# A hybrid decoder layer: the row statistics of the first norm from a second reading of x, another order for the first tile, and three biases on ScalarE

## The chip, the cores and the metric

The kernel runs on one core of one Trainium2 chip. The core has five engines with a queue each, and every engine works through its queue in order: PE (TensorE, matrix products), DVE (VectorE), ACT (ScalarE), POOL (GpSimd) and SP (SyncE, which here only issues transfers). PEld is PE's loading of the stationary operand, which overlaps its products. The metric is the time of one execution on the device, in microseconds (us). Lines such as L1411 are lines of the kernel before.

## The reference

One layer of a causal decoder trunk, sequence 1024, model width 1024, float32. Only the first part matters here:

```python
mod = silu(c) @ W_ada + b_ada            # shift, scale, gate for each of two sub-layers
y = x * rsqrt(mean(x * x, axis=-1) + EPS) * g_mix
u = y * (1 + scale1) + shift1
proj = u @ w_in                          # q, k, v, u_ssm, two gates
```

Behind it follow dilated window attention over eight heads, a state space branch, gates, an output projection, a second modulated norm, a convolutional gated MLP and a final norm.

## The kernel before

Everything is kept transposed: channels on the 128 partitions, tokens along the row. `xs[k]` (k = 0 to 7) is tile k of x, 128 channels by 1024 tokens, and `halves` are its two halves of 512 tokens. Precision comes from splitting each operand into a high and a low part (`xg[k][:, 0]` and `xg[k][:, 1]`, the same for weights): `mm3` (L186 to L188) is three products, high by high, high by low, low by high.

The first stage does not wait for the norm's root. A tile of x needs only its gain `gs1`, which a dot of a row block of `w_ada` with silu(c) gives (`row_dot`, `ada_dot`, DVE, L1427). So loop `k` (L395) multiplies the unnormed, scaled tile by the columns of four weight tiles (first q, first k, two of the state space input) into seven PSUM banks `b0`: seven `mm3` per k, 21 products. `prep_a(k)` makes the gain and ACT's high part (L323), `prep_b(k)` DVE's low part (L376); both run one and two tiles ahead. The root comes in later, when `scale_r` multiplies the banks by `rr` (L432), the reciprocal root of the mean square, held on all partitions.

That root is built here from `square(k)` (ACT, L350), summed over the tiles by DVE (L352), and from `stats(h2)` (L381): a product with a matrix of -1 sums over the partitions and spreads the sum to all of them, and `rsqrt_of` takes the root on ACT with one Newton step on DVE (L1395 to L1400), for 512 tokens at a time. The first half is done inside tile 7, the second in the V stage.

The shift needs eight more dots (row blocks 0 to 7, loaded late, L402), then `shl` (L448 to L450), and PE's products for a bias row (L458, L459). The bias is added to the scaled banks by POOL (`add_bias0`, L483). The V stage (L537 to L576) then makes `u` per tile and half: `mod_a` is DVE then ACT (L1405, L1406), `mod_b` DVE (L1411). Its first half covers tokens 0 to 511 for all eight k, its second half the rest, and between the products of the second half the first q and k parts are split (`put_q`, `put_k`), V is stored (`put_v`), and the next weights are split (`Weights`, ACT L122 and POOL L123).

The order is written out by hand: the program order of each engine is the order of the calls below, and waits are put in where data or a buffer is needed. `late` says before which (tile, bank) of the loop a step is called. All loads go through SP's queue, in the order of the calls; a load waits for its buffer, and everything behind it waits as well. Pages of 8 KB per partition (`b.A`, 17 of them) hold rows of `w_ada`, `xg`, `u` and more. Before the loop PE runs `WARM` dummy products (L281).

Of the kernel before, what the change touches and what calls it, by code (L numbers as in the profile page):

```python
# [10 lines left out]
F32 = mybir.dt.float32  # L11
# [37 lines left out]
QHI = ((-5, -3, 0, 2, 3, 5, 6), (-7, -5, -2, 0, 12, 2, 17))  # L49
EPS = 1e-6  # L50
BIG = 1e30
WARM = 26
DOTS = ((5, 3), (5, 6), (6, 1), (6, 3), (7, 2), (7, 2), (7, 3), (7, 5))
STATS = ((7, 0),)
NEWTON = ((7, 2),)
A2PACE, A2AHEAD, A2DELAY = 8.0, 2, 0.0
LEAD, FILL_PACE, SCORE_PACE = 9, 1.55, 1.2
SLOW_PACE, LAST_PACE, SLOW_END = 1.52, 0.5, 60
# [152 lines left out]
def body(tc, I, O, dbg=None):  # L211
    b = Builder(tc, I, O)
    nc = tc.nc
    with ExitStack() as ctx:
# [87 lines left out]

        def split_w(i):
            raw = raws.pop(i)
            w = b.whl.tile([P, 2, 1024], R32, name="whl", tag="whl") if i in (0, 1, 5) else b.A([P, 2, 1024], R32, "whA")
            for cs in halves if i == 0 else [slice(0, 1024)]:
                nc.scalar.activation(w[:, 0, cs], raw[:, cs], AF.Copy)
                nc.vector.tensor_sub(w[:, 1, cs], raw[:, cs], w[:, 0, cs].bitcast(F32))
                if i == 0:
                    xg_hi(0, [halves[1]] if cs.start == 0 else [])  # L310
            return w

        def split_hi(i):
# [21 lines left out]
        for k in range(3):  # L335
            load_x(k)
        nc.sync.dma_start(spar, I["spar"])
        sqp = b.A([P, 2, S], F32, "sq")
        b0 = {k: b.ps(tag) for k, tag in zip(((1, 0), (2, 0), (0, 0), (3, 0), (1, 1), (2, 1), (0, 1)),
                                             ("s", "s", "t", "t", "mm", "mm", "o"))}  # L340
        w0, xg = [], {}

        base = pg1.tile([P, KT], F32, name="base")
        nc.vector.tensor_scalar(base, cols[:, KT:2 * KT], 1.0, None, op0=OP.add)
        lag1 = []

        def square(k):

            sq = sqp[:, 1 if k else 0]
            nc.scalar.activation(sq, xs[k], AF.Square)  # L350
            if k:
                lag1.append(lambda: nc.vector.tensor_add(sqp[:, 0], sqp[:, 0], sq))  # L352

        def prep_a(k):
            low = None
            if k and k % 2 == 0:
                w, low = split_hi(k // 2)
                w0.append(w)
            row_dot(KT + k)
            nc.vector.tensor_scalar(gs1[:, k:k + 1], mod[:, KT + k:KT + k + 1], base[:, k:k + 1],  # L360
                                    cols[:, C_GMIX + k:C_GMIX + k + 1], op0=OP.add, op1=OP.mult)
            if k == 0:
                xg_hi(0, halves[:1])
                w0.append(split_w(0))
            else:
                xg_hi(k, [slice(0, S)])
            if low:
                low()
            for fn in lag1:
                fn()  # L370
            lag1.clear()
            square(k)

        def prep_b(k):
            for hs in halves if k == 0 else [slice(0, S)]:
                nc.vector.scalar_tensor_tensor(xg[k][:, 1, hs], xs[k][:, hs], gs1[:, k:k + 1],  # L376
                                               xg[k][:, 0, hs].bitcast(F32), op0=OP.mult, op1=OP.subtract)

        newton = {}

        def stats(h2):  # L381
            sps = b.ps("o")
            nc.tensor.matmul(sps, b.nones, sqp[:, 0, halves[h2]], start=True, stop=True)
            newton[h2] = rsqrt_of(b, rr[:, halves[h2]], sps)
            next(newton[h2])

        late = {}
        for fn, at in ((row_dot, DOTS), (stats, STATS), (lambda h2: list(newton[h2]), NEWTON)):
            for a, kn in enumerate(at):
                late.setdefault(kn, []).insert(0, (fn, a))  # L390
        prep_a(0)
        prep_b(0)
        load_x(3)
        prep_a(1)
        for k in range(KT):  # L395
            if k + 4 < KT:
                load_x(k + 4)
                if k + 4 in (4, 6):
                    load_w((k + 4) // 2)
            elif k < 7:  # L400
                for j in range(3 * (k - 4), min(3 * (k - 4) + 3, KT)):
                    load_row(j)  # L402
            if k + 1 < KT:
                prep_b(k + 1)
            if k + 2 < KT:
                prep_a(k + 2)
            elif k == 6:
                lag1.pop()()
                load_w(4)
                load_w(5)  # L410
            o = (k % 2) * 512
            for n, ((t, hf), ps) in enumerate(b0.items()):
                w = w0[k // 2][:, :, o + t * P:o + (t + 1) * P]
                for fn, a in late.get((k, n), []):
                    fn(a)
                b.mm3(ps, w[:, 0], w[:, 1], xg[k][:, 0, halves[hf]], xg[k][:, 1, halves[hf]], k == 0, k == KT - 1)
                b.unit(0.65)
            del xg[k]
# [23 lines left out]
        def u_half(k, hf, *between):  # L442
            u_a(k, hf)
            scale_r(*between)
            u_b(k, hf)
# [34 lines left out]

        def add_bias0(t, hf):
            x = t0.pop((t, hf))
            nc.gpsimd.tensor_scalar(x, x, 1.0, bias0[:, t:t + 1], op0=OP.mult, op1=OP.add)  # L483
            return x

        usd = [b.dram.tile([P, T, J], F32, name=f"usd{q}") for q in range(2)]
# [50 lines left out]
        for hf in range(2):  # L537
            for k in range(KT):
                if hf == 0:
                    if k % 2 == 0 and k < 6:  # L540
                        wv.append(split_w(5 + k // 2))
                        if k == 0:
                            load_w(7)
                    if 1 < k + 1 < KT:
                        u.append(b.A([P, 2, S], R32, "u"))
                        u_half(k + 1, 0, *{3: [(1, 1)], 4: [(2, 1)], 5: [(0, 1)]}.get(k, []))
                    if k == 1:
                        stats(1)
                    if k == 2:
                        list(newton[1])  # L550
                    if k == 5:
                        bias_cols()
                    if k == 7:
                        u_half(0, 1)
                        u_a(1, 1)
                else:
                    if k == 0:
                        qk_tiles(0)
                    put = put_q(0, k, add_bias0(0, k)) if k < 2 else put_k(0, k - 2, add_bias0(1, k - 2)) if k < 4 \
                        else put_v(k - 4)  # L560
                    if k + 1 < KT:
                        u_b(k + 1, 1)
                    next(put)
                    if k + 2 < KT:
                        u_a(k + 2, 1)
                    list(put)
                    xs[k] = None
                    if k == 3:
                        us0 = [(t - 2, hf, add_bias0(t, hf)) for t, hf in ((2, 0), (2, 1), (3, 0))]
                    if k in (3, 6):  # L570
                        W.prefetch(k // 3)
# [3 lines left out]
                          wv[k // 2][:, 0, o:o + 512], wv[k // 2][:, 1, o:o + 512], k == 0, k == KT - 1)  # L575
                    b.unit(0.65)  # L576
            if hf == 0:
                del sqp
                vps += [b.ps(t) for t in ("mm", "mm", "o", "o")]
        p1.close()  # L580
        wv = None
# [1280 lines left out]
def layout(x, c, w_ada, b_ada, g_mix, w_in, b_gate, a_re, a_im, log_dt, b_re, b_im, c_re, c_im, d_skip,  # L1862
           w_glu, b_glu, w_proj_att, w_proj_ssm, w_out, g_ffn, w_up, w_conv, b_conv, w_down, g_final):
    A = np.ascontiguousarray
    a = {}
    a["xT"] = A(x[0].T).reshape(KT, P, S)
    a["c"] = c
    a["wada"] = A(w_ada[0].T)
    win = w_in[0]
# [43 lines left out]
```

## Time and profile before

| | us |
|---|---|
| median of three runs | 1168.1 (1165.98 to 1169.69) |
| the profiled execution: its time | 1168.23 |
| its span | 1166.4 |
| PE busy | 1113.7 (95%) |
| DVE busy | 883.3 (76%) |
| ACT busy | 574.0 (49%) |
| POOL busy | 158.5 (14%) |
| bytes moved | 155.00 MB, 133 GB/s in the mean |

Times in rows count from the start of the span. A row of a timeline has start, duration, engine, line, operation, written and read tiles, and in brackets the idle time before it and what ended that. Rows of products overlap, so that a row of 0.39 us can be followed by the next after 0.23. A row of PE's waits has what waited, for whom, the total, how often, and the longest.

### The profile page before, as it was taken

Reading aid. Unit: us, or ns where it says so; the run is one execution under the profiler, and the core shown is the slowest. Engines: PE = TensorE matmul, PEld = TensorE weight load, DVE = VectorE, ACT = ScalarE, POOL = GpSimd, SP = SyncE. Lnnn points to the kernel's source line nnn. Section 1 sums busy time; section 2 is a strip of 40 time slices with the busy share of each in tenths; the row PEclk is TensorE's granted clock in tenths of the full one; section 3 lists DMA queues with packets and bytes.
Section 4 is the critical chain, followed back from the end, with each engine's and each line's share of the span. In section 5 each row is a group of like instructions: output and inputs, shape, how many; then the busy total and the mean of one; then the engine's idle time right before and its main releaser. Section 6 shows DMA issues by size and latency. Waiting matters only on the chain.

```text
span 1166.4 us, 14714 instructions
## 1 busy us (share of the span) xinstructions
PE 1113.7 (95%) x5276; PEld 916.2 (79%) x5276; DVE 883.3 (76%) x1681; ACT 574.0 (49%) x1039; POOL 158.5 (14%) x178
## 2 busy tenths in 40 slices
PE   8899999999999996999999999999999999999995
PEld 7767888888878885878778887788888888887884
DVE  6989687776568796248867779888877768879777
ACT  5436777778832312333334565443445336735653
POOL 1012444445421311100000000000000000000003
PEclk8999999999999998999999999999999999999998
DMA  9411111111022220244584351245324337779333
GB/s 367 195 54 43 68 46 37 48 44 64 11 81 73 59 89 27 73 163 153 188 299 154 98 227 65 91 158 206 131 89 140 114 108 271 248 273 360 129 127 144
DMA packets 56184, 155.00 MB, mean 133 GB/s; under 512 B 7312, under 2 KB 13584, under 8 KB 54320
## 3 DMA queue, kind: packets, MB, share of 16 engines
q1 hardware_dynamic: 46368, 140.37, 33.9%
q10 hardware_dynamic: 9744, 13.70, 3.7%
q8 instruction: 41, 0.67, 0.2%
q14 instruction: 31, 0.25, 0.1%
HBM read 122.00 MB, written 31.46 MB: 132 GB/s over the span
## 4 chain that ended last, share of the span: by engine, by line
PE 66%; DVE 18%; ACT 8%; DMA 5%; issue 3%; SPq 0%; DVEq 0%; ACTq 0%
PE ps_s L1273 12%; PE ps_mm L1273 9%; PE ps_mm L186 7%; PE ps_mm L188 7%; PE ps_mm L187 7%; PE ps_t L1273 7%; PE ps_s L187 3%; PE ps_s L186 3%; PE ps_s L188 3%; PE ps_t L1566 2%; PE ps_s L1530 1%; PE ps_o L1583 1%; ACT op L833 1%; PE ps_s L1531 1%; DMA hd<-h 1%
## 5 line engine op out<-in xcount | busy, mean ns | idle before, releaser
L1273 PE MATMUL ps_s<-op,half 128*128 128x512 f32 x792 | 189.7, 390 | 4.0 <-ACT ps_s L1287 1.8
L1273 PEld LDWEIGHTS ps_s<-op,half 128*128 128x128 f32 x792 | 148.1, 188 | 37.1 <-ACT ps_s L1287 2.9
L186 PE MATMUL ps_mm<-u,whl 128*128 128x512 f32 x360 | 143.9, 400 | 0.7 <-ACT tp L1830 0.7
L188 PE MATMUL ps_mm<-u,whl 128*128 128x512 f32 x360 | 140.8, 391 | 0.0
L187 PE MATMUL ps_mm<-u,whl 128*128 128x512 f32 x360 | 140.6, 390 | 0.0
L1273 PE MATMUL ps_mm<-op,half 128*128 128x512 f32 x528 | 127.2, 393 | 2.2 <-DVE f L978 2.0
L1273 PEld LDWEIGHTS ps_mm<-op,half 128*128 128x128 f32 x528 | 100.1, 190 | 23.9 <-ACT half L1078 2.4
L1273 PE MATMUL ps_t<-op,half 128*128 128x512 f32 x432 | 103.9, 389 | 0.7 <-ACT tp L1281 0.7
L1273 PEld LDWEIGHTS ps_t<-op,half 128*128 128x128 f32 x432 | 81.0, 188 | 17.9 <-ACT tp L1281 1.1
L1375 POOL TENSOR_TENSOR hh<-hh,acc 128x512 f32<-128x512 f32 x3 | 4.2, 1439 | 650.2 <-DVE acc L1400 650.2
L123 POOL TENSOR_TENSOR whl<-wraw,whl 128x256 fp32r<-128x256 f32 (+2 forms) x52 | 63.8, 1227 | 140.4 <-ACT whl L122 134.0
L188 PEld LDWEIGHTS ps_mm<-u,whl 128*128 128x128 f32 x360 | 67.6, 188 | 14.8
L186 PEld LDWEIGHTS ps_mm<-u,whl 128*128 128x128 f32 x360 | 67.8, 188 | 12.7 <-ACT tp L1830 1.2
L187 PEld LDWEIGHTS ps_mm<-u,whl 128*128 128x128 f32 x360 | 67.8, 188 | 10.5
L1571 DVE TENSOR_TENSOR PT<-ps_t,PT 128x512 fp32r<-128x512 f32 (+1 forms) x80 | 50.6, 633 | 27.9 <-ACT PT L1569 27.4
L1079 DVE TENSOR_TENSOR half<-scr,half 128x512 fp32r<-128x512 f32 x80 | 54.5, 684 | 16.2 <-ACT half L1078 16.2
L122 ACT ACTIVATE whl<-wraw 128x256 fp32r<-128x256 f32 (+2 forms) x73 | 49.7, 681 | 26.6 <-PE ps_s L188 19.0
L1542 ACT ACTIVATE S<-S,mcol 128x128 f32<-128x128 f32 (+3 forms) x64 | 49.3, 771 | 14.5 <-DVE mcol L1540 12.9
L1546 POOL TENSOR_SCALAR S<-S,mcol 128x128 f32<-128x128 f32 (+3 forms) x64 | 48.6, 761 | 50.2 <-DVE mcol L1545 34.9
L1078 ACT ACTIVATE half<-scr 128x512 fp32r<-128x512 f32 x80 | 49.0, 626 | 8.2 <-DVE scr L1060 5.8
L1079 DVE TENSOR_TENSOR half<-wraw,half 128x512 fp32r<-128x512 f32 x66 | 44.9, 684 | 7.2 <-ACT half L1078 7.1
L1569 ACT ACTIVATE PT<-ps_t 128x512 fp32r<-128x512 f32 (+1 forms) x80 | 43.7, 550 | 10.3 <-PE ps_t L1566 9.2
(496 smaller groups left out, 2448.0 us busy)
## 6 DMA issues: line engine op xcount, KB each, us to landing
wraw<-in_wup SPq DMA_DIRECT2D x32, 512.0 KB, 3.6
fq<-f SPq DMA_DIRECT2D x16, 1024.0 KB, 5.3
ft<-fq SPq DMA_DIRECT2D x14, 1024.0 KB, 7.8
ada<-in_wada SPq DMA_DIRECT2D x24, 512.0 KB, 8.8
wraw<-in_wdn SPq DMA_DIRECT2D x20, 512.0 KB, 5.7
adaB<-in_wada ACTq DMA_DIRECT2D x16, 512.0 KB, 3.6
wraw<-in_wout SPq DMA_DIRECT2D x16, 512.0 KB, 3.6
hd<-h SPq DMA_DIRECT2D x12, 512.0 KB, 6.7
```

Source lines behind the costliest of these rows:

```text
L122: nc.scalar.activation(w[:, 0, cs], raw[:, cs], AF.Copy)
L123: lo.tensor_sub(w[:, 1, cs], raw[:, cs], w[:, 0, cs].bitcast(F32))
L186: nc.tensor.matmul(ps, wh, xh, start=first, stop=False)
L187: nc.tensor.matmul(ps, wh, xl, start=False, stop=False)
L188: nc.tensor.matmul(ps, wl, xh, start=False, stop=last)
L1078: nc.scalar.activation(w[:, 0], src, AF.Copy)
L1079: lows.append(lambda: nc.vector.tensor_sub(w[:, 1], src, w[:, 0].bitcast(F32)))
L1273: mm = lambda wp, xp, i: nc.tensor.matmul(ps, w[:, wp, ws], xp[:, cs], start=first and k + i == 0, stop=k == KT // 2 - 1 and i == 2, skip_ ...
L1542: nc.scalar.activation(tl, tl, AF.Exp, bias=mc[:, 0:1], scale=-1.0, accum_out=mc[:, 2:3])
L1546: nc.gpsimd.tensor_scalar(tl, tl, mc[:, 3:4], 0.0, op0=OP.mult, op1=OP.add)
L1569: nc.scalar.activation(pt[:, 0, :w], tps[:, :w], AF.Copy)
L1571: 0, lambda: nc.vector.tensor_sub(pt[:, 1, :w], tps[:, :w], pt[:, 0, :w].bitcast(F32)))
```

## The change

The mean square no longer comes from the transposed tiles. x is given a second time as `xn`, with tokens on partitions (the host passes the same array without the transpose); eight tiles of 128 tokens by 1024 are loaded in loop steps 2 to 5, two per step, into four half pages, and ACT squares each in place and gives the sum along the row into one column of `ssq` (`accum_out`). The root is then taken once, for 128 x 8 numbers, at tile 7, bank 0. Since token t's root now stands in one partition, `spread_a` scales the identity matrix by a column of it, four times for a half, and `spread_b` multiplies by the matrix of -1, which puts the (negated twice) values along the row on all partitions; ACT copies them to `rr`. The first half is spread at banks 2 and 5 of tile 7, the second in steps 0 and 1 of the V stage. The first tile gets a function of its own, in which DVE makes the low part of `xg` ahead of the low part of the weights, and the second half of the weights' low part only after `prep_a(1)`. The dots of the shift stand at other places, WARM goes from 26 to 31, and the three tiles' biases are added by ACT.

```diff
-WARM = 26
-DOTS = ((5, 3), (5, 6), (6, 1), (6, 3), (7, 2), (7, 2), (7, 3), (7, 5))
-STATS = ((7, 0),)
-NEWTON = ((7, 2),)
+WARM = 31
+DOTS = ((5, 3), (5, 6), (6, 1), (6, 3), (6, 5), (7, 1), (7, 3), (7, 4))
...
-        sqp = b.A([P, 2, S], F32, "sq")
+        xnp = {}
+        ssq = pg1.tile([P, 2, KT], F32, name="ssq")
...
+        def load_xn(n):
+            if n in (0, 2):
+                page = b.A([P, 2, D], F32, "xn")
+                xnp[n], xnp[n + 1] = page[:, 0], page[:, 1]
+            nc.sync.dma_start(xnp[n % 4], I["xn"][n])
+
+        def square(n):
+
+            nc.scalar.activation(xnp[n % 4], xnp[n % 4], AF.Square, accum_out=ssq[:, 0, n:n + 1])
...
             if low:
                 low()
-            for fn in lag1:
-                fn()
-            lag1.clear()
-            square(k)
...
+        def prep_first():
+
+            row_dot(KT)
+            nc.vector.tensor_scalar(gs1[:, 0:1], mod[:, KT:KT + 1], base[:, 0:1], cols[:, C_GMIX:C_GMIX + 1],
+                                    op0=OP.add, op1=OP.mult)
+            xg_hi(0, halves[:1])
+            raw = raws.pop(0)
+            w = b.whl.tile([P, 2, 1024], R32, name="whl", tag="whl")
+            w0.append(w)
+            for hs in halves:
+                nc.scalar.activation(w[:, 0, hs], raw[:, hs], AF.Copy)
+                if hs.start == 0:
+                    xg_hi(0, halves[1:])
+            low = lambda hs: nc.vector.tensor_sub(w[:, 1, hs], raw[:, hs], w[:, 0, hs].bitcast(F32))
+            prep_b(0, halves[:1])
+            low(halves[0])
+            prep_b(0, halves[1:])
+            return lambda: low(halves[1])
+
+        def root(_):
+
+            q, r = ssq[:, 0], ssq[:, 1]
+            nc.scalar.activation(r, q, AF.Abs_reciprocal_sqrt, bias=b.epsc, scale=1.0 / D)
+            t = b.tp()[:, :KT]
+            nc.scalar.activation(t, r, AF.Square, scale=math.sqrt(0.5 / D))
+            nc.vector.scalar_tensor_tensor(t, q, EPS * D, t, op0=OP.add, op1=OP.mult)
+            nc.vector.scalar_tensor_tensor(r, t, -1.5, r, op0=OP.add, op1=OP.mult)
+
+        diag = {}
+
+        def spread_a(h2):
+            diag[h2] = b.tp()
+            for i in range(4):
+                nc.scalar.activation(diag[h2][:, i * P:(i + 1) * P], ident, AF.Copy, scale=ssq[:, 1, 4 * h2 + i:4 * h2 + i + 1])
+
+        def spread_b(h2):
+
+            ps = b.ps("o")
+            nc.tensor.matmul(ps, b.nones, diag.pop(h2), start=True, stop=True)
+            nc.scalar.activation(rr[:, halves[h2]], ps, AF.Copy)
...
-        for fn, at in ((row_dot, DOTS), (stats, STATS), (lambda h2: list(newton[h2]), NEWTON)):
+        for fn, at in ((row_dot, DOTS), (root, ((7, 0),)), (spread_a, ((7, 2),)), (spread_b, ((7, 5),))):
...
-        prep_a(0)
-        prep_b(0)
+        rest = prep_first()
         load_x(3)
         prep_a(1)
+        rest()
...
-            elif k < 7:
+            if 2 <= k < 6:
+                for n in (2 * k - 4, 2 * k - 3):
+                    if n > 3:
+                        square(n - 4)
+                    load_xn(n)
+            if 4 <= k < 7:
                 for j in range(3 * (k - 4), min(3 * (k - 4) + 3, KT)):
                     load_row(j)
...
             elif k == 6:
-                lag1.pop()()
+                for n in range(4, KT):
+                    square(n)
                 load_w(4)
                 load_w(5)
...
-            nc.gpsimd.tensor_scalar(x, x, 1.0, bias0[:, t:t + 1], op0=OP.mult, op1=OP.add)
+            nc.scalar.activation(x, x, AF.Identity, bias=bias0[:, t:t + 1])
...
+                    if k == 0:
+                        spread_a(1)
                     if k == 1:
-                        stats(1)
-                    if k == 2:
-                        list(newton[1])
+                        spread_b(1)
...
     a["xT"] = A(x[0].T).reshape(KT, P, S)
+    a["xn"] = A(x[0]).reshape(KT, P, D)
```

More of the change, by code (lines that the diff above doesn't have):

```diff
@@ L304, in split_w @@
             raw = raws.pop(i)
[L305 to L310, printed above, removed]
+            w = b.whl.tile([P, 2, 1024], R32, name="whl", tag="whl") if i == 5 else b.A([P, 2, 1024], R32, "whA")
+            nc.scalar.activation(w[:, 0], raw, AF.Copy)
+            nc.vector.tensor_sub(w[:, 1], raw, w[:, 0].bitcast(F32))
             return w
@@ L344, in body @@
         nc.vector.tensor_scalar(base, cols[:, KT:2 * KT], 1.0, None, op0=OP.add)
[L345 to L352, printed above, removed]
+        def load_xn(n):
[5 more added lines that the diff above has]
+            nc.scalar.activation(xnp[n % 4], xnp[n % 4], AF.Square, accum_out=ssq[:, 0, n:n + 1])
         def prep_a(k):
             low = None
-            if k and k % 2 == 0:
+            if k % 2 == 0:
                 w, low = split_hi(k // 2)
@@ L361, in prep_a, with prep_b @@
                                     cols[:, C_GMIX + k:C_GMIX + k + 1], op0=OP.add, op1=OP.mult)
[L362 to L366, printed above, removed]
+            xg_hi(k, [slice(0, S)])
             if low:
                 low()
-            for fn in lag1:
-                fn()
-            lag1.clear()
-            square(k)
-        def prep_b(k):
-            for hs in halves if k == 0 else [slice(0, S)]:
+        def prep_b(k, parts=(slice(0, S),)):
+            for hs in parts:
@@ L376, in prep_b @@
                 nc.vector.scalar_tensor_tensor(xg[k][:, 1, hs], xs[k][:, hs], gs1[:, k:k + 1],
                                                xg[k][:, 0, hs].bitcast(F32), op0=OP.mult, op1=OP.subtract)
[L379 to L385, printed above, removed]
+        def prep_first():
[15 more added lines that the diff above has]
+            return lambda: low(halves[1])
@@ L577, in body @@
             if hf == 0:
-                del sqp
+                del xnp
                 vps += [b.ps(t) for t in ("mm", "mm", "o", "o")]
```

## The prediction

> **What bounds the kernel now.** I read the page first, then busy time by stretch, then what PE waited for, then the timelines of the first 120 us, the only part that the change touches.
>
> ```profile
> span 1166.4 us, 14714 instructions
> ...
> 13.00:19.00 6.00, 5.83 (x14) 4.57 (x15) 4.71 (x9) 3.04 (x3) 0.00 (x0) 0.50 1.03 415
> 25.00:30.00 5.00, 5.00 (x24) 4.14 (x23) 4.87 (x7) 3.44 (x4) 0.00 (x0) 1.00 1.03 420
> 40.00:45.00 5.00, 5.00 (x24) 4.14 (x23) 4.96 (x8) 3.40 (x4) 0.00 (x0) 1.00 0.56 226
> 55.00:60.00 5.00, 1.75 (x8) 0.67 (x9) 4.90 (x12) 0.00 (x0) 0.00 (x0) 1.00 0.00 0
> ```
>
> The columns are PE, PEld, DVE, ACT and POOL busy (with counts), granted clock, DMA share, GB/s. The profiled run took 1168.23 us, 1.8 beside its span; the median of the three runs is 1168.1, so sums against one hold for the other. From 25 to 40 three things are full at once: PE, DVE, and the DMA engines (1.03, 420 GB/s). At 55 only DVE is.
>
> ```profile
> PE ps_o L458 <- DVE shl L450: 3.3, 1, 3.3
> PE ps_mm L188 <- DVE u L1411: 2.9, 2, 2.6
> PE ps_s L187 <- DVE xg L376: 2.0, 1, 2.0
> ```
>
> PE's three longest waits up to 160 us are all on DVE: at the first tile, at the bias row (L458), and in the second half of V. These are what the change can win.
>
> ```profile
> 1.05 8.13 PE L282 MATMUL ps_o<-nones 128*128 128x128 f32 x52 [1.05 <-DVE epsc L271]
> ...
> 10.63 0.69 DVE L308 TENSOR_TENSOR whl<-wvx,whl 128x512 fp32r<-128x512 f32 x1 [1.31 <-ACT whl L307]
> 10.65 0.50 PE L186 MATMUL ps_s<-xg,whl 128*128 128x512 f32 x1 [1.48 <-ACT whl L307]
> ...
> 12.38 1.41 DVE L376 SCALAR_TENSOR_TENSOR xg<-xk,gs,xg 128x512 fp32r<-128x512 f32 x2
> ...
> 13.18 0.79 PE L187 MATMUL ps_s<-xg,whl 128*128 128x512 f32 x1 [2.03 <-DVE xg L376]
> ...
> 13.70 1.22 DVE L1427 CUSTOM_DVE_ANT_0 ada<-ada,cpage 128x1024 f32<-128x1024 f32 x1
> ...
> 16.45 1.28 DVE L376 SCALAR_TENSOR_TENSOR xg<-xk,gs,xg 128x1024 fp32r<-128x1024 f32 x1 [1.22 <-ACT xg L323]
> ```
>
> **Part 1, the first tile.** DVE made both low halves of the weights before the low part of xg. In the new order it makes xg's low half 0 first: its input is ready at 10.1, so it ends at 10.8; weights' low half 0 ends at 11.5, xg's low half 1 at 12.1. PE then issues at 10.65, 10.9 and 11.5 and goes on. The clock row for 13 to 19 shows 0.50 after PE had stood nearly idle from 9.2 to 13.2; 14 matmuls there took 0.43 each, against 0.227 at the full clock (24 rows in 5 us from 25 to 30, two of them reaching in from outside). With WARM at 31, five more dummy products at 8.13/26 (0.31 at most) end at about 10.5, and PE hardly pauses. So the 21 matmuls of tile 0 end near 15.8 instead of 20.6: 4.8 us earlier on PE. The DVE dot of tile 1 moves from 13.70 to 12.0 and its xg low part from 16.45 to 14.8; PE waits 0.1 for it.
>
> **Part 2, the squares leave the tiles.** Eight ACT squares and seven DVE adds of 1.22 go out of the eight tiles. After that DVE needs per tile a dot 1.2, its gain 0.3, ACT's high part 1.15 (in whose shadow the weights' low part lies) and the low part 1.28: 3.9, against 21 x 0.227 = 4.8 for PE. The xg low parts then start at 14.8, 18.7, 22.7, 26.7, 30.7 and 35.4, always ahead of PE, which starts tile 7 at about 44.6.
>
> ```profile
> 21.51 0.33 SPq L331 DMA_DIRECT2D x<-in_xT  x1
> 22.74 9.26 SPq L293 DMA_DIRECT2D ada<-in_wada  x8
> ...
> 59.36 0.33 SPq L300 DMA_DIRECT2D wvx<-in_wv  x1
> ```
>
> The DMA answers for the last x tile, the last of these eight rows, and that lone transfer (last number: us from issue to landing):
>
> ```profile
> x<-in_xT SPq DMA_DIRECT2D x1, 512.0 KB, 10.2
> ```
> ```profile
> ada<-in_wada SPq DMA_DIRECT2D x1, 512.0 KB, 10.0
> ```
> ```profile
> wvx<-in_wv SPq DMA_DIRECT2D x1, 512.0 KB, 3.4
> ```
>
> **Part 3, the eight loads of xn.** They are new: 4.19 MB on the same SP queue, between the x tiles and the eight late rows of w_ada. x7 lands at 21.51 + 10.2 = 31.7, the last row (issued at 31.7, the end of its group less 0.33) at 41.7: eight rows in 10.0 us, 1.25 each, which is 0.524 MB at 420 GB/s. DMA was already full, so these loads lie beside nothing: all that is behind them lands 10.0 us later. With 0.4 more (the second weight tile waits for the postponed low half 1 of the first), row 0 lands at 40.9, xn7 at 45.9, rows 3 to 7 at 47.1 to 52.1, and the first V weights at 53.4 instead of 42.8. SP also holds xn4 to xn7 behind ACT squares 0 to 3. These end at 31.9, 33.1, 36.7 and 38.4, while five or six transfers are still under way (SP runs eight ahead), so I price that hold at 0; a queue found empty would cost 3.4 instead of 1.25 each time. The x tiles behind xn0 to xn3 slip too (x7 to 34.6, used at 38).
>
> ```profile
> 44.10 1.28 ACT L1395 ACT_TABLE_LOAD   x1
> ...
> 49.14 1.02 PE L383 MATMUL ps_o<-sq,nones 128*128 128x512 f32 x2
> ...
> 50.20 0.69 ACT L1395 ACTIVATE rr<-ps_o,epsc 128x512 f32<-128x512 f32 x1 [4.82 <-PE ps_o L383]
> ...
> 52.31 0.69 DVE L1400 SCALAR_TENSOR_TENSOR rr<-tp,rr 128x512 f32<-128x512 f32 x1
> ...
> 56.36 1.22 DVE L1427 CUSTOM_DVE_ANT_0 ada<-ada,cpage 128x1024 f32<-128x1024 f32 x1
> ...
> 58.25 0.40 PE L458 MATMUL ps_o<-whl,shl 128*2 128x512 f32 x1 [3.29 <-DVE shl L450]
> ```
>
> **Part 4, the end of the tiles.** Before, the last dot started at 56.36 because DVE was full, and PE went on 1.9 later. Now the dots wait for rows. Dots 0 and 1 run at 40.9 and 42.1, and behind them waits the low part of tile 7 (43.3 to 44.5, just when PE asks). Dots 3 and 4 run at 47.1 and 48.4; the root's two DVE steps follow. On ACT the last square starts when xn7 lands and takes 1.25 (below), the table load 1.28, two tiny activations about 0.4: 48.9, hidden by dot 4. DVE finishes the root at 50.1, ACT's four diagonals take about 0.9, and PE's spreading product starts near 51.05. PE reached it at 48.1, so it stands still for 3 us and ends tile 7 at 53.5. Dots 5, 6, 7 end the chain: row 7 at 52.1, dot at 52.4, bias row at 52.4 + 1.9 = **54.3**, 3.9 before the old 58.25. So the 4.8 of part 1 and the DVE time of part 2 are mostly spent waiting for rows. The product itself costs what the old one did.
>
> ```profile
> 43.02 1.06 ACT L350 ACTIVATE sq<-x 128x1024 f32<-128x1024 f32 x1
> ```
> ```profile
> L1542 ACT ACTIVATION_READ_ACCUMULATOR S<-S,mcol 128x1 f32 x64 | 12.0, 187 | 0.0
> ```
>
> A square with a sum has no row. Bounds: 1.06, and 1.06 + 0.19 if the sum is read out as at L1542; I take 1.25. The four diagonals (128x128) lie between 0.76 (four V copies, below) and four times 0.4; I take 0.9, and up to 0.7 more is covered by dots 5 to 7.
>
> ```profile
> 62.00:88.00 26.00, 25.03 (x103) 17.90 (x102) 20.40 (x29) 10.38 (x15) 5.29 (x6) 1.00 0.12 42
> 88.00:113.40 25.40, 22.52 (x98) 17.84 (x96) 23.46 (x47) 16.01 (x44) 6.60 (x4) 1.00 0.07 21
> ```
> ```profile
> 82.71 6.87 POOL L483 TENSOR_SCALAR t<-t,bias 128x512 f32<-128x512 f32 x7 [77.56 <-DVE bias L477]
> 102.39 2.62 POOL L123 TENSOR_TENSOR whl<-wraw,whl 128x1024 fp32r<-128x1024 f32 x1 [12.81 <-ACT whl L122]
> ```
> ```profile
> 84.96 1.18 DVE L1405 SCALAR_TENSOR_TENSOR xk<-xk,gs,rr 128x512 f32<-128x512 f32 x1
> ...
> 90.47 0.74 DVE L1405 SCALAR_TENSOR_TENSOR xk<-xk,gs,rr 128x512 f32<-128x512 f32 x1
> ...
> 102.83 2.72 DVE L1411 SCALAR_TENSOR_TENSOR u<-xk,mod,u 128x512 fp32r<-128x512 f32 x1
> ...
> 118.00 0.29 DVE L1533 CUSTOM_DVE_ANT_0 S<-ps_s,near 128x128 f32<-128x128 f32 x1 [2.31 <-DMA near<-in_bt]
> ```
> ```profile
> 91.25 0.72 ACT L1406 ACTIVATE u<-xk,mod 128x512 fp32r<-128x512 f32 x1 [0.31 <-DVE xk L1405]
> ...
> 102.21 0.76 ACT L495 ACTIVATE V<-ps_s 128x128 fp32r<-128x128 f32 x4
> ```
>
> **Part 5, the V stage.** It starts 3.6 to 3.9 earlier as a whole: the first V weights at 53.4 give ACT 1.0 and DVE 1.2 until 55.7, where the first modulation came at 59.25 before. Of its 51.4 us, 192 matmuls at 0.227, the product's 1.1 and small ones of 0.7 need 45.4; 6.0 are PE's waits, 2.4 in the first half and 3.6 in the second. The change touches them in four ways. The second half's two root steps (0.69 each) leave DVE, and ACT's two (0.69 and 0.63) are replaced by four diagonals and one copy of about the same sum. The seven biases leave POOL: while they ran, DVE steps took 1.18 for 0.74 and 0.99 for 0.75, four steps or 1.35 in all. DVE is thus some 2.7 us earlier at the second half. ACT takes seven steps of 0.72 (5.0), three of them together ahead of the split of the next weights; it is busy 16.0 of 25.4 us there, so I price it at 0 to 1. PE's waits of the first half then shrink by about 1.3, those of the second by about 2.3 of 2.9, since u at 102.83 falls ahead of POOL's step of 2.62 instead of under it.
>
> Two losses stand against this. The POOL step itself stays, and hits another DVE step. And the next weights' load waits for that POOL step, and the table `near` for that load; the first scores already wait 2.31 for `near`, and as V shrinks these come some 1.1 us later against PE. Net gain of the stage: 1.3 + 2.3 - 1.1 = **2.5**, with bounds from -1 (no wait shrinks, 1.1 lost) to 4.5.
>
> The Trainium skill, page "SBUF — State Buffer", section "Who interferes with whom", says that a DVE instruction with two SBUF inputs and a GpSimd instruction that reads SBUF exclude each other, and that the second one blocks. The trace agrees at 102.83 (2.72 beside a POOL step of 2.62). By that rule alone each of the four DVE steps could have waited up to a whole POOL step, 0.98, or 3.9 in all; the rows show 1.35, and the sum goes by them.
>
> **Sum.** 1168.2 - 3.9 - 2.5 = **1161.8 us**. From the attention on the same programs run behind the same orders, so the shift stays.
>
> **Rivals.**
>
> A: V gives nothing. PE gets 3.9 at the bias row, but DVE's 2.7 us meet ACT's new steps, or the POOL step falls on another u that PE needs. For it: the second half's DVE is busy 23.46 of 25.4. Against: the worst wait is one collision, and every DVE step before it moves. 1168.2 - 3.9 = 1164.3.
>
> B: PE's clock falls in the new gap. PE stands from 48.1 to 51.05 and again from 53.5 to 54.3; after the idle stretch from 9.2 to 13.2 it ran at 0.50 for some 14 matmuls, 0.2 us lost on each, 2.8. Against: after the 3.3 us wait before 58.25 the row from 55 to 60 shows 1.00. 1161.8 + 2.8 = 1164.6. The Trainium skill, page "TensorE: Matmul & The Clock Gate", section "Part 1: The HAM clock gate (the "warmup" mystery)", puts the limit at about 3.4 us of idle and the recovery at as much busy time. By that rule the new gap would just pass; the trace agrees so far.
>
> C: the rows eat everything. If the rows land 4 us later than by 1.25 each (an xn transfer slower than a w_ada one, or a page of row 4 or 6 freed late), the bias row stands where it did and V as well: 1168.2. For it: nothing hides this load.
>
> D, slower: SP holds. If SP's waits for ACT squares 0 to 3 let the queue run dry each time, every one of xn4 to xn7 costs 3.4 - 1.25 = 2.15 for the lone transfer and 1.25 for the square ahead of it: 4 x 3.4 = 13.6. The bias row comes at 67.9 instead of 58.25, 9.7 later; V returns 2.5: 1168.2 + 9.7 - 2.5 = 1175.4. It decides from 3.9 + 2.5 + 3.5 = 9.9 us of lost queue on. Against it are the five transfers under way.
>
> **How the numbers follow.** Forecast 0.58, A 0.16, B 0.06, C 0.12, D 0.08. This kernel's runs spread from 1165.98 to 1169.69, so less than 0.3% (3.5 us: 1164.6 to 1171.6) is no change. The forecast, with its own range 1159.3 (V gives 4.5, 0.5 for row landing) to 1163.5, is faster; A lies 0.3 beyond the border and B on it, so of these 0.22 I give 0.12 to faster and 0.10 to no change; C is no change, D slower. Faster 0.70, same 0.22, slower 0.08. The range 1159 to 1167.5 leaves out D and most of C.
>
> **What would show it.** The profile after should have PE's first tile without the 2.0 wait and a granted clock of 1.00 from 13 to 19; DMA full until about 54; a PE wait near 48 for the diagonals and a short one for the bias row; the bias row at 54.3; no POOL before 90; V's end 6 to 8 us earlier than 113.4. I am wrong in part 3 if the last row lands far from 52, in part 4 if dots run before their rows are the limit, in part 5 if V's second half still has its 2.6 us wait on u.

## The result, and the profile after

The changed kernel takes 1160.55 us, the median of four runs (1159.33 to 1161.57), against 1167.7 for the kernel before, run beside it (1165.98 to 1169.69). The ratio is 0.9935 with an interval of [0.9923, 0.9948]: faster by 0.65%, or 7.15 us by the medians. 1161.8 was forecast. The profiled execution took 1159.33, the quickest of the four, 8.9 less than the profiled one of before. One execution of the biases alone and one of the change without its biases, both further down, were slowed throughout (granted clock 0.75 and 0.65); they are left out of the medians, and since the first of them is the profiled one, no trace of the biases alone is read.

Line numbers moved with the change: `mm3` is now L184 to L186, the square L350, the root's ACT steps L391 and L393, the four diagonals L402, the spreading product L407, the bias row L487 and L488, the bias addition L512, `mod_a` L1434 and L1435, `mod_b` L1440.

The page's first line of after, and busy time by stretch of after (columns as before: PE, PEld, DVE, ACT, POOL with counts, granted clock, DMA share, GB/s):

```profile
span 1157.5 us, 14754 instructions
```
```profile
13.00:19.00 6.00, 6.00 (x28) 4.82 (x27) 5.25 (x8) 3.26 (x3) 0.00 (x0) 1.00 1.03 419
...
40.00:45.00 5.00, 5.00 (x24) 4.14 (x23) 4.81 (x7) 1.83 (x4) 0.00 (x0) 1.00 1.02 419
45.00:50.00 5.00, 2.64 (x12) 1.86 (x10) 3.47 (x7) 3.64 (x9) 0.00 (x0) 1.00 1.03 418
50.00:55.00 5.00, 4.34 (x11) 2.27 (x12) 4.48 (x11) 2.27 (x5) 0.00 (x0) 0.71 0.52 211
55.00:60.00 5.00, 4.84 (x21) 2.21 (x19) 4.62 (x8) 2.90 (x5) 0.00 (x0) 0.94 0.32 108
62.00:88.00 26.00, 26.00 (x117) 21.09 (x116) 20.40 (x30) 14.11 (x22) 0.00 (x0) 1.00 0.13 41
```

In the first tile PE has twice the products of before in 13 to 19, at the full clock. The DMA engines stay full past 50, 10 us longer than before: 226 GB/s stood in 40 to 45 then, 419 now. Between 45 and 50 PE has nothing to do for half the time. From 62 to 88, most of it V's first half, PE is full, where 25.03 of 26 were before, and POOL does nothing.

What PE waited for up to 160 us in after (total, times, longest):

```profile
PE ps_o L407 <- ACT tp L402: 3.0, 1, 3.0
PE ps_mm L184 <- DVE V L527: 1.1, 1, 1.1
...
PE ps_mm L186 <- DVE u L1440: 0.5, 1, 0.5
```

Of the three waits of before, the first tile's 2.0 and the bias row's 3.3 are gone, and of V's 2.9 on `u` 0.5 is left. In their place stand the spreading product's wait for the diagonals and a wait at V's end that before did not have. PE's timeline of after shows where these lie:

```profile
10.11 0.51 PE L184 MATMUL ps_s<-xg,whl 128*128 128x512 f32 x1 [0.31 <-ACT whl L379]
10.46 0.42 PE L185 MATMUL ps_s<-xg,whl 128*128 128x512 f32 x1
10.98 0.50 PE L186 MATMUL ps_s<-xg,whl 128*128 128x512 f32 x1
...
47.25 0.39 PE L186 MATMUL ps_mm<-xg,whA 128*128 128x512 f32 x1
50.66 1.12 PE L407 MATMUL ps_o<-tp,nones 128*128 128x512 f32 x2 [3.03 <-ACT tp L402]
...
53.75 0.63 PE L487 MATMUL ps_o<-whl,shl 128*2 128x512 f32 x1
...
58.28 0.40 PE L184 MATMUL ps_s<-whA,u 128*128 128x512 f32 x1
...
105.82 0.47 PE L184 MATMUL ps_mm<-u,whl 128*128 128x512 f32 x1 [1.09 <-DVE V L527]
```

The two rows of before's timeline that answer to the last two, V's first product and the first one behind V:

```profile
61.97 0.40 PE L186 MATMUL ps_s<-whA,u 128*128 128x512 f32 x1
...
113.45 0.47 PE L186 MATMUL ps_mm<-u,whl 128*128 128x512 f32 x1
```

The first product starts at 10.11 here and at 10.65 before. Over the traces read here it lies anywhere from 9.48 to 10.95, so times are best counted from it. The bias row comes 53.75 - 10.11 = 43.64 after it, against 58.25 - 10.65 = 47.60: **3.96 earlier**. From the bias row to the first product behind V it is 105.82 - 53.75 = 52.07, against 113.45 - 58.25 = 55.20: **3.13 less**. Together that is 7.1, which is what the medians show. The two profiled executions differ by 8.9: 0.5 more is the earlier first product, and 1.3 lies behind V, where the programs are the same. Over seven of the traces the time from the first product behind V to the end goes from 1048.8 to 1053.0, so nothing is read from that remainder.

The DMA answer for the tile of the new loads in after (durations in ns, least, median, most; the last line is from issue to landing), and ACT's and DVE's timelines around the end of the tiles:

```profile
L350 ACT ACTIVATE xn<-xn x8: 1042/1061/1062, 30.2 to 45.2; 128x1024 f32<-128x1024 f32 x8
L350 ACT ACTIVATION_READ_ACCUMULATOR xn<-xn x8: 183/185/187, 31.2 to 46.1; 128x1 f32 x8
...
DMA to landing us min/median/max: 6.2/8.7/10.5
```
```profile
45.17 1.06 ACT L350 ACTIVATE xn<-xn 128x1024 f32<-128x1024 f32 x1
46.14 0.18 ACT L350 ACTIVATION_READ_ACCUMULATOR xn<-xn 128x1 f32 x1
46.34 1.28 ACT L391 ACT_TABLE_LOAD   x1
...
49.33 1.28 ACT L402 ACTIVATE tp<-ident,ssq 128x128 f32<-128x128 f32 x4 [1.15 <-DVE ssq L395]
...
102.24 1.06 ACT L120 ACTIVATE whl<-wraw 128x1024 fp32r<-128x1024 f32 x1 [0.80 <-DMA wraw<-in_wk]
```
```profile
40.19 1.22 DVE L1456 CUSTOM_DVE_ANT_0 ada<-ada,cpage 128x1024 f32<-128x1024 f32 x1 [2.75 <-DMA ada<-in_wada]
...
46.42 1.23 DVE L1456 CUSTOM_DVE_ANT_0 ada<-ada,cpage 128x1024 f32<-128x1024 f32 x1 [1.42 <-DMA ada<-in_wada]
...
53.12 0.17 DVE L479 TENSOR_TENSOR shl<-mod,shl 128x8 fp32r<-128x8 f32 x1
...
97.80 1.55 DVE L1440 SCALAR_TENSOR_TENSOR u<-x,mod,u 128x512 fp32r<-128x512 f32 x1
...
110.32 0.29 DVE L1562 CUSTOM_DVE_ANT_0 S<-ps_s,near 128x128 f32<-128x128 f32 x1 [2.28 <-DMA near<-in_bt]
```

DVE, which was full before, now stands twice for late rows of `w_ada`. ACT goes straight from the last square to the root, and its diagonals wait for DVE's last root step. At 102.24 ACT stands 0.80 for the load of the next weights, with V's last copies queued behind it; the first scores wait 2.28 for `near`, as they did before (2.31).

### The profile page after: what moved, and what is told of

Same layout as the page of the kernel before. It is cut to its first block, busy times and chain, and to the rows that moved or that the text cites. A ratio compares the mean times of both kernels' runs of the same rounds, so it can differ in the third digit from the quotient of the medians.

```text
span 1157.5 us, 14754 instructions
## 1 busy us (share of the span) xinstructions
PE 1109.4 (96%) x5286; PEld 914.5 (79%) x5286; DVE 871.7 (75%) x1672; ACT 581.2 (50%) x1062; POOL 151.7 (13%) x171
## 4 chain that ended last, share of the span: by engine, by line
PE 67%; DVE 18%; ACT 8%; DMA 5%; issue 3%; SPq 0%; DVEq 0%; ACTq 0%
PE ps_s L1302 13%; PE ps_mm L1302 10%; PE ps_t L1302 8%; PE ps_mm L184 7%; PE ps_mm L186 7%; PE ps_mm L185 7%; PE ps_s L184 2%; PE ps_s L185 2%; PE ps_s L186 2%; PE ps_t L1595 2%; DMA xk<-in_xT 2%; DMA xn<-in_xn 1%; PE ps_s L1559 1%; DVE op L866 1%; PE ps_o L1612 1%
## 5 line engine op out<-in xcount | busy, mean ns | idle before, releaser
L184 PE MATMUL ps_mm<-u,whl 128*128 128x512 f32 x360 | 143.9, 400 | 1.8 <-DVE V L527 1.1
L186 PE MATMUL ps_mm<-u,whl 128*128 128x512 f32 x360 | 140.8, 391 | 0.0
L186 PEld LDWEIGHTS ps_mm<-u,whl 128*128 128x128 f32 x360 | 67.6, 188 | 14.8
L184 PEld LDWEIGHTS ps_mm<-u,whl 128*128 128x128 f32 x360 | 67.7, 188 | 13.9 <-issue 2.2
```

The source lines that it names most:

```text
L184: nc.tensor.matmul(ps, wh, xh, start=first, stop=False)
L186: nc.tensor.matmul(ps, wl, xh, start=False, stop=last)
```

## The experiments

Two readings of the 4 us at the bias row were open. **Q**, the prediction's own: the late rows of `w_ada` and DVE's dots on them set the bias row, so that tile 0's earlier start is spent in waiting. **S**: the earlier start carries the gain. **V** stands for part 5's account of the V stage. All times are medians, and all ratios are to the kernel before, run on the same chip; the kernels were not all run on one chip, so they are compared by their ratios.

| kernel | us | ratio |
|---|---|---|
| the change | 1160.55 | 0.9935 [0.9923, 0.9948] |
| first tile alone | 1165.91 | 0.9989 [0.9977, 1.0001] |
| biases alone | 1164.65 | 0.9978 [0.9965, 0.9992] |
| statistics alone | 1163.37 | 0.9962 [0.9950, 0.9975] |
| change without its first tile | 1159.71 | 0.9935 [0.9919, 0.9952] |
| change without its biases | 1162.23 | 0.9954 [0.9937, 0.9971] |
| change with one load of xn | 1156.54 | 0.9907 [0.9888, 0.9926] |
| change with the gap filled | 1160.30 | 0.9937 [0.9919, 0.9954] |
| sums on PE, no xn | 1158.45 | 0.9918 [0.9900, 0.9935] |
| change, split later | 1161.49 | 0.9952 [0.9940, 0.9963] |
| sums on PE, split later | 1160.71 | 0.9941 [0.9925, 0.9957] |
| sums on PE, `near` earlier | 1157.08 | 0.9915 [0.9902, 0.9929] |
| sums on PE, `near` earlier, split later | 1156.31 | 0.9906 [0.9891, 0.9921] |

**The first tile alone.** The kernel before with the new order and 31 dummy products.

```diff
-WARM = 26
+WARM = 31
...
-        prep_a(0)
-        prep_b(0)
+        rest = prep_first()
         load_x(3)
         prep_a(1)
+        rest()
```

> The kernel before with the first tile's new order and WARM 31 alone. Theory Q (the dots of the shift set the end of the tiles; whatever PE wins before is spent waiting there): DVE keeps its seven adds and its full queue and starts only 1.7 us earlier (dot of tile 1 from 13.7 to 12.0), so the bias row comes near 56.5 instead of 58.25 and PE's wait for it grows from 3.3 to about 6: 1167.7 - 1.7 = 1166.0 us. Rival S (PE's start reaches the end): 1167.7 - 4.8 = 1162.9 us.

1165.91, a ratio of 0.9989 whose interval takes in 1: the time of Q, not of S. PE's timeline of this kernel, and its stretch from 55 to 60:

```profile
51.58 0.39 PE L188 MATMUL ps_o<-xg,whA 128*128 128x512 f32 x1
55.27 0.59 PE L478 MATMUL ps_o<-whl,shl 128*2 128x512 f32 x1 [3.30 <-DVE shl L470]
55.65 0.63 PE L479 MATMUL ps_o<-whl,shl 128*1 128x512 f32 x1
...
61.59 0.39 PE L186 MATMUL ps_s<-whA,u 128*128 128x512 f32 x1
```
```profile
55.00:60.00 5.00, 4.73 (x12) 1.39 (x13) 4.62 (x8) 1.44 (x2) 0.00 (x0) 0.50 0.33 105
```

PE still stands 3.3 us for the bias row, where I expected about 6, and the row comes 55.27 - 10.64 = 44.63 after the first product, 3.0 earlier than before: more than the 1.7 of Q, less than the 4.8 of S. But the clock then fell to 0.50, and from the bias row to V's first product it took 6.32 instead of 61.97 - 58.25 = 3.72: 2.6 of the 3.0 were gone at once. The rest went in V, where PE's 2.9 on `u` stayed and the clock fell once more behind it (0.66 from 105 to 110, 1.00 in before): the first product behind V starts at 113.56, against 113.45 before. So Q had the time right, but mostly by way of the clock, which it did not contain; what the earlier start would bring alone if the clock did not fall was not run.

**The change without its first tile.**

```diff
-WARM = 31
+WARM = 26
...
+                nc.vector.tensor_sub(w[:, 1, hs], raw[:, hs], w[:, 0, hs].bitcast(F32))
...
-            low = lambda hs: nc.vector.tensor_sub(w[:, 1, hs], raw[:, hs], w[:, 0, hs].bitcast(F32))
-            prep_b(0, halves[:1])
-            low(halves[0])
-            prep_b(0, halves[1:])
-            return lambda: low(halves[1])
+            prep_b(0, halves)
...
-        rest = prep_first()
+        prep_first()
...
-        rest()
```

> The changed kernel with the old order of the first tile and WARM 26. Theory Q: the last row of w_ada still lands near 52, PE reaches the spreading product later and waits less for it, the bias row stays within 1 us of its place: 1160.6 to 1161.5 us. Rival S: the first tile's 4.3 to 4.8 us come back: 1165 us.

1159.71, the ratio of the change itself. S falls. PE's timeline of this kernel:

```profile
50.87 1.08 PE L404 MATMUL ps_o<-tp,nones 128*128 128x512 f32 x2
...
53.58 0.39 PE L483 MATMUL ps_o<-whl,shl 128*2 128x512 f32 x1 [0.24 <-DVE shl L475]
```

With the old first tile PE comes to the spreading product later and just in time, without the wait, and the bias row stands at 53.58, where it stands in the change (53.75). What PE loses in the first tile here, it stands still for there, from 47.6 to 50.66. In this trace the clock from 13 to 19 was 0.75, and not 0.50 as in before. Where it was 0.50, in the statistics alone below, the bias row comes 55.63 - 10.89 = 44.74 after the first product, 1.1 later than in the change; so the new first tile may be worth up to about 1 us, which these medians cannot tell from nothing.

**The change with one load of xn.** Only the first of the eight loads is made, and all eight squares read it, so every block of 128 tokens gets the first block's mean squares.

```diff
-            nc.sync.dma_start(xnp[n % 4], I["xn"][n])
+            if n == 0:
+                nc.sync.dma_start(xnp[0], I["xn"][0])
...
-            nc.scalar.activation(xnp[n % 4], xnp[n % 4], AF.Square, accum_out=ssq[:, 0, n:n + 1])
+            nc.scalar.activation(xnp[1], xnp[0], AF.Square, accum_out=ssq[:, 0, n:n + 1])
```

> The changed kernel with one of the eight loads of xn; all eight squares read that tile, so every root is that of the first 128 tokens. Theory Q: everything behind lands 7 x 1.25 = 8.8 us earlier, the squares and the root are long done, PE does not stop at the spreading product, the bias row follows PE and DVE near 49.8 instead of 53.75: 1160.55 - 4 = 1156.6 us, with DMA idle from about 45. Rival (not the transfers but the chain square, root, diagonal, or DVE itself, holds the end): 1160 us or more.

1156.54, 4.0 below the change. PE's timeline of this kernel:

```profile
48.11 1.02 PE L408 MATMUL ps_o<-tp,nones 128*128 128x512 f32 x2
...
50.35 0.40 PE L488 MATMUL ps_o<-whl,shl 128*2 128x512 f32 x1
```

No wait is left at either product, and the bias row comes 50.35 - 10.75 = 39.60 after the first product, 4.0 earlier than in the change. By the ratios it is 3.3 us ahead of the change, and the two intervals just overlap. This is the direct price of the other seven loads, and it is what the prediction said is "mostly spent waiting for rows".

**Sums on PE, no xn.** The rival design: ACT squares the transposed tiles into fp32r (the squares are rounded to it), and PE sums them over channels and tiles, eight products for each half of the tokens, the first eight inside the tiles and the other eight in V. No square is added by DVE, and nothing is loaded for it. First tile and biases are as in the change.

```diff
...
+            nc.scalar.activation(sq0[k], xs[k][:, halves[0]], AF.Square)
...
+            nc.scalar.activation(sq1[k], xs[k][:, halves[1]], AF.Square)
...
+            nc.tensor.matmul(st0, n32, sq0.pop(k), start=k == 0, stop=k == KT - 1)
...
+                for k in range(KT):
+                    nc.tensor.matmul(sps, n32, sq1.pop(k), start=k == 0, stop=k == KT - 1)
...
```

> No second reading of x: ACT squares the transposed tiles, rounded to fp32r (so the mean square is a little less exact), and PE sums them over partitions and tiles with eight products for each half of the tokens, which replaces DVE's seven adds; first tile and biases as changed. Theory Q: rows land near 42 as before, DVE has no adds, PE does not wait; the bias row comes near 51 instead of 53.75 at full clock, V starts 3 us earlier, and V gives back 0.7 for its eight products and up to 1 for the root steps on DVE: 1157 to 1159.5 us. Rival: DVE or the root's chain takes over: 1160.6 us or more.

1158.45, as expected. The bias row in this kernel:

```profile
51.48 0.40 PE L478 MATMUL ps_o<-whl,shl 128*2 128x512 f32 x1
```

It comes 51.48 - 10.82 = 40.66 after the first product, 3.0 earlier than in the change; the eight products in V, 0.23 each, take back up to 1.8 of that. The medians differ by 2.1, but the two intervals overlap, so this alone does not show it faster than the change. It does show that the gain does not need the second reading of x. How much of it is the squares' leaving DVE and how much the new first tile, which is in this kernel too and whose time PE does not wait away here, was not run.

**The biases: alone, and undone in the change.** One line each, the one on top of the kernel before, the other taken out of the change.

```diff
-            nc.gpsimd.tensor_scalar(x, x, 1.0, bias0[:, t:t + 1], op0=OP.mult, op1=OP.add)
+            nc.scalar.activation(x, x, AF.Identity, bias=bias0[:, t:t + 1])
```

> The kernel before with the biases on ACT alone. Theory V: the four DVE steps that took 1.18 and 0.99 take 0.74 and 0.75, DVE is 1.35 us earlier at the second half, and u at 102.83 falls ahead of POOL's split: PE's 2.9 us of waits for u shrink by 1.4 to 2.6: 1165.1 to 1166.3 us. Rival (ACT's seven steps take the place of POOL's): 1167.7 us or more.

> The changed kernel with the seven biases back on POOL. Theory V (POOL's steps hold DVE's, and push u under the split of the next weights): DVE loses about 1.35 us around 77 to 84 and PE waits for u again in the second half of V: 1162 to 1163.5 us. Rival (V won by the root steps that left DVE alone): 1160.6 us, DVE's lag disappearing in its slack.

Alone: 1164.65, 2.8 less than the 1167.47 beside it, 0.45 below the range that V gave. Undone: 1162.23, 1.7 more than the change and inside V's range; the intervals of the two overlap, so it is the trace that shows what the biases on POOL cost. With the biases back on POOL, one of PE's waits, a step of DVE and one of POOL read:

```profile
PE ps_mm L186 <- DVE u L1440: 2.6, 1, 2.6
```
```profile
97.13 2.72 DVE L1440 SCALAR_TENSOR_TENSOR u<-xk,mod,u 128x512 fp32r<-128x512 f32 x1
```
```profile
96.69 2.62 POOL L121 TENSOR_TENSOR whl<-wraw,whl 128x1024 fp32r<-128x1024 f32 x1 [12.81 <-ACT whl L120]
```

The collision of before is back, on the same `u`: it starts under the split's step and takes 2.72. In the change DVE is further on, the next `u` meets only the end of POOL's step (1.55 at 97.80), and PE waits 0.5. DVE's four steps beside POOL's biases take 1.00, 1.18, 0.98 and 1.18 again, where the same steps take 0.74 to 0.75 in the change. From the bias row to the first product behind V the kernel with the biases back takes 107.75 - 54.52 = 53.23, which is 1.2 more than the change and 2.0 less than before. So the biases are some 1.2 of the 3.1 won there, and the rest came with the other parts.

**Statistics alone.** The change with the old first tile and the biases on POOL.

```diff
-WARM = 31
+WARM = 26
...
-        rest = prep_first()
+        prep_first()
...
-            nc.scalar.activation(x, x, AF.Identity, bias=bias0[:, t:t + 1])
+            nc.gpsimd.tensor_scalar(x, x, 1.0, bias0[:, t:t + 1], op0=OP.mult, op1=OP.add)
```

> The changed kernel with the old first tile and the biases on POOL: only the statistics from xn, with the new places of the dots, are left. Theory Q: the bias row still comes near 53.6 to 54, and V has only the root steps off DVE, as with the biases undone: 1162 to 1162.6 us, the same as with the biases undone alone. Rival S: 1166 us.

1163.37: 0.8 above what Q expected, 2.6 below what S did. The bias row comes at 55.63, later than expected (the first product of this trace, at 10.89, is late as well). The 2.6 us wait on `u` is there, and behind it the clock fell to 0.66 (100 to 105), where it stayed at 1.00 with the biases undone. The three parts alone give 0.11, 0.22 and 0.38%, 0.71 in sum, and together 0.65 [0.52, 0.77]: they add up within the intervals, with the first tile's share not told from zero.

**The gap filled.** Twelve small dummy products ahead of the first spreading product, to keep PE busy while it waits.

```diff
+FILL = 12
...
+            for _ in range(FILL if h2 == 0 else 0):
+                nc.tensor.matmul(ps[:, :P], b.nones, b.nones, start=True, stop=True)
```

> The changed kernel with twelve dummy products ahead of the first spreading product, in the 3.0 us in which PE waits for the diagonals. If the idle time is what drops the clock after 52, the granted clock stays 1.00 and the nine products at 0.43 take 0.23: PE starts V 1.2 us earlier (then DVE's u is the limit): 1159.4 to 1160.1 us. If the clock falls for another reason, or V's start is DVE's anyway: 1160.6 us.

The clock stays up, but the time, 1160.3, does not move. The stretch from 50 to 55, and PE's timeline at the start of V:

```profile
50.00:55.00 5.00, 3.92 (x16) 1.95 (x15) 4.32 (x10) 2.34 (x5) 0.00 (x0) 1.00 0.46 188
```
```profile
53.73 0.39 PE L490 MATMUL ps_o<-whl,shl 128*2 128x512 f32 x1 [0.47 <-DVE shl L482]
...
57.42 0.39 PE L185 MATMUL ps_s<-whA,u 128*128 128x512 f32 x1
...
58.78 0.50 PE L185 MATMUL ps_s<-whA,u 128*128 128x512 f32 x1 [0.51 <-DVE t L464]
```

The bias row now waits 0.47 for `shl`, V's first product comes at 57.42 instead of 58.28, and three products on stands a new wait of 0.51 for DVE's `t`. Counted from the first product of all, V's fourth stands at 58.78 - 9.86 = 48.92 here and at 58.98 - 10.11 = 48.87 in the change: nothing is won. So, as far as one trace can show it, standing idle lowered the clock, and in the change the half clock hides behind DVE. My expectation, that the lost time would come back, missed.

**The wait at V's end.** PE's 1.1 there came from ACT's split of the next weights, which waits for their load ahead of V's last copies. I put the split one step later.

```diff
-                    if k in (3, 6):
+                    if k in (3, 7):
```

> The changed kernel with the split of the second next weights one step later in V (k = 7 for 6), so that ACT's copies of V no longer stand behind a split that waits for its load. Theory: PE's wait of 1.1 us at the end of V (for V's low parts) goes, but POOL's split, the load behind it and the table near come up to 1 us later, and the first scores wait for that table anyway: 1159.5 to 1160.6 us. If the table binds, nothing is won; if the wait was a plain loss, 1159.5.

Slower than expected, 1161.49, though the interval overlaps with that of the change. PE's waits in this kernel, DVE's first score step, and the issue of the load of `near`, first here and then in the change:

```profile
PE ps_s L1559 <- DVE mcol L1562: 2.1, 2, 1.8
...
PE ps_mm L184 <- DVE V L527: 0.5, 1, 0.5
```
```profile
112.59 0.29 DVE L1562 CUSTOM_DVE_ANT_0 S<-ps_s,near 128x128 f32<-128x128 f32 x1 [4.67 <-DMA near<-in_bt]
```
```profile
106.88 0.38 SPq L616 DMA_DIRECT2D near<-in_bt  x1
```
```profile
106.20 0.38 SPq L616 DMA_DIRECT2D near<-in_bt  x1
```

The wait at V's end fell from 1.1 to 0.5, and the first scores wait 4.67 for `near` instead of 2.28. Its load stands on SP's queue behind one that waits for POOL's split. Counted from the first product it is issued as in the change (106.88 - 10.95 = 95.93, against 96.09), while V ends 1.0 earlier: that is one part of the longer wait. The other, 1.5, is that the load took 5.5 us to land instead of 4.0. It took 5.7 with the gap filled and 5.4 with the sums on PE, where no split was moved; why, these runs leave open. The same move on the kernel with the sums on PE:

> The kernel with the sums on PE (squares rounded to fp32r) and the later split together: 1158.45 us less what the later split is worth, 0 to 1.1: 1157.4 to 1158.5 us.

1160.71, by the medians slower again, with intervals that overlap: `near` is waited for 6.30 there, and took 7.2 to land. So the load of `near` was put ahead of it in that kernel, at tile 5 of V's second half, without and with the later split.

```diff
+                    if k == 5:
+                        near = b.B([P, 2, HF], F32, "near")
+                        nc.sync.dma_start(near[:, 0], I["bt"][0, :, HF:])
...
-        near = b.B([P, 2, HF], F32, "near")
...
-        nc.sync.dma_start(near[:, 0], I["bt"][0, :, HF:])
```

> The kernel with the sums on PE (squares rounded to fp32r) and, in addition, the load of the table near at step 5 of V's second half, ahead of the load that waits for POOL's second split. Theory N (with a shorter V the first scores wait for near, 3.70 us of idle DVE there in that kernel and 1.1 us of PE behind it): near lands before 104, DVE's first score step starts with PE's scores, PE's waits of 0.8 to 1.1 for it go: 1158.45 - 0.5 to 1.5 = 1157 to 1158 us. Rival (far or the tables behind it bind next): 1158.5 us.

> The same with the second split one step later. That split alone made near later and lost about 2 us; with near loaded ahead of it, theory N has nothing left to lose there and wins the 0.7 to 1.2 us at the end of V: 1156 to 1157.5 us. Rival (the split itself, not near, was what cost 2 us): 1160 us.

1157.08 and 1156.31. With both, the first score step and PE's wait at V's end read:

```profile
107.61 0.29 DVE L1554 CUSTOM_DVE_ANT_0 S<-ps_s,near 128x128 f32<-128x128 f32 x1 [1.65 <-PE ps_s L1552]
```
```profile
PE ps_mm L184 <- DVE V L518: 0.5, 1, 0.5
```

DVE now waits for PE's scores and not for a load. Against the same kernel with `near` late this is 4.4 us, with the intervals apart. It is the quickest kernel here by the median; its interval, [0.9891, 0.9921], lies just below that of the change. Without the split moved, the gain of `near` alone cannot be told from the kernel with the sums on PE.

## Why the prediction was right, point by point

**The forecast** came 1.25 us too high, inside its own range, and with the right cause in the main. 0.5 of the 1.25 is that the kernel before stood at 1167.7 beside the change and not at 1168.2; 0.6 is part 5. By its parts:

**Part 1** held. The three products of tile 0 issue at 10.11, 10.46 and 10.98 where 10.65, 10.9 and 11.5 were given, and the clock in 13 to 19 is 1.00. That this is "mostly spent waiting for rows" is borne out by undoing it: the time does not change by more than its noise.

**Part 2** held: the low parts of xg for the tiles 1 to 6 start at 14.26, 18.23, 22.19, 26.15, 30.11 and 34.71, each 0.5 to 0.7 ahead of what was given, 0.5 of it by the earlier start, and PE waits for none of them.

**Part 3** held with its sizes. A square with its sum takes 1.06 and a read of 0.19, the upper of the two bounds and the value taken. The last x tile's load was issued at 24.0 and took 9.9, to land at 33.9 where 34.6 was given. The last row, issued at 41.4 and 10.0 on its way, landed near 51.4 for 52.1. The hold of SP behind the squares costs nothing: the quickest load of xn took 6.2 us from issue to landing, nearly twice the 3.4 of a lone transfer, and the DMA share stays at 1.02 to 1.03 from 25 to 50, so the queue did not run dry. That is **rival D** gone, and **rival C** with it, since the rows came when they should. The seven loads cost 4.0 us by experiment.

**Part 4** held within half a microsecond: PE reached the spreading product at 47.6 and waited 3.0 (48.1 and 3 given), started it at 50.66 (51.05), and the bias row came 3.96 earlier for 3.9. The four diagonals took 1.28 where I took 0.9, so nearer the upper bound of 1.6, and the dots behind them covered it. The short wait that I expected ahead of the bias row is not there, because PE, slowed by its clock, arrived last.

**Part 5** is the term that was mis-sized: 3.1 instead of 2.5. The first half's waits are nearly gone (26.00 of 26 busy from 62 on), and 0.5 of the second half's 2.9 is left. The 3.1 already bears a loss that the sum did not have: the half clock holds back V's start by 0.8 (58.28 - 53.75 = 4.53 behind the bias row, against 3.72), and V itself is 3.9 shorter (47.54, against 51.48). What the sum then takes off, 1.1 for `near`, came at another place. The scores wait 2.28 for `near` in the change and 2.31 before, no more. It is the load of the next weights, which the prediction saw only as what `near` stands behind, that is late first: ACT waits 0.80 for it ahead of V's copies, and PE waits 1.1 at V's end. The amount is right by chance; the chain is the one that the prediction named, one link earlier. With the later split the link after it shows: ACT's wait shrinks, V ends earlier, and the scores wait longer for `near`.

**Rival A** falls by the same 3.1, and by the biases alone, whose interval leaves out 1.

**Rival B** had its mechanism right and its price wrong, and my reason against it was wrong. I held the row of before, 3.29 us of idle time and a clock of 1.00 behind it, to show that a 3 us gap would pass. In the change the clock fell in just that gap, to 0.71 in 50 to 55. The price, 2.8, is 2.6 where PE sets the pace (the first tile alone) and nothing here, where DVE's `t` is as late. That the forecast stood without this price is luck. The Trainium skill, page "TensorE: Matmul & The Clock Gate", section "Part 1: The HAM clock gate (the "warmup" mystery)", gives a limit of about 3.4 us and says that the activity window runs free of the kernel. The limit, as I used it, does not agree with this trace, which shows the fall after 3.03 us. The recovery, which the prediction put at as much busy time, took longer in the first tile of before: products ran at half clock from 13.18 to 19.0, for 5.8 us. That the outcome differs between gaps of one length fits the free window, and no run here tests it.

## What to carry to other kernels

Before a stage is made faster, ask which load its last step needs and where that load stands in its queue: here a quicker first tile won nothing that could be told from noise beside rows that came later, and seven loads bought to relieve an engine cost 4.0 us of what they gave. Sums over partitions that PE makes from data on the chip can stand in for a second reading: here they were no slower, and 2.1 us quicker by the medians. And where a stage shrinks, a small load that stands last on the shared queue can be the next wait: here, to take away the wait ahead of it gained nothing until that load was moved as well.

## What the runs showed of the hardware that was not expected

The clock falls after less idle time than I thought, and not always. PE stood 3.03 us in the change, 3.30 with the first tile alone, 3.28 with the biases undone and 2.70 with the split later, and each time products then ran at half clock for three to six microseconds (granted clock 0.71 and, for the last two, 0.66 from 50 to 55; 0.50 from 55 to 60 with the first tile alone). In the kernel before it stood 3.29, and nothing fell. The waits of 2.6 on `u` in V show the same: the clock fell behind them with the first tile alone and with the statistics alone (0.66 both times), and stayed at 1.00 in before and with the biases undone. The length of the gap alone does not decide; what does, these runs leave open. In the change the fall came late: products ran 0.43 apart from 52.47 on, 1.8 us after PE had started again at 50.66, to 55.46. In the three others they were slow within 0.6 us. With small dummy products in the gap the one trace taken shows 1.00.

The same load of 256 KB, `near`, issued at the same place in the program, took 4.0 us to land in the change and 4.1 in before, 5.4 to 5.7 in three other kernels, and 7.2 in one. These runs do not show why.
